# A decoder layer's projection units: even row lengths for the meta operand tiles, another order of the block products, stores by halves

## The chip, the cores and the metric

The kernel runs on one core of a Trainium2 chip. The metric is the device time of one execution in microseconds. The kernel before takes 993.65 us, the median of three runs (993.39 to 994.78).

## What is computed

One layer of a decoder trunk on 1024 tokens and 16 learned meta tokens in front of them, 1024 channels, all in float32:

```
h = rms_norm(h_res, pre_norm_g)
z = h @ w_in                                  # 1024 x 7328
(pv, pg, cq, ckv, kr, mg, cu, cg, sbcx, sg, gl) = split_cols(z)
y_a = (pool_mixer(pv) * silu(pg)) @ w_out_pool
y_b = (mla_attention(cq, ckv, kr) * silu(mg)) @ w_out_mla
y_c = (conformer_conv(cu) * silu(cg)) @ w_out_conf
y_d = (short_conv(sbcx) * silu(sg)) @ w_out_sc
gts = sigmoid(gl + gate_bias)                 # four gates of 1024 channels
m = gts[0]*y_a + gts[1]*y_b + gts[2]*y_c + gts[3]*y_d
h_res = h_res + rms_norm(m @ w_o, post_norm_g)
```

The convolution branch starts with a gated linear unit: `a, gate = split(cu)`, `a * sigmoid(gate)`, then a causal depthwise convolution of width 31, a layer norm and a swish. The meta tokens are dropped at the end.

## The kernel before, in words

The kernel has three stages: the input projection with all that can be made from it beside (about 643 us), attention with three of the output projections, and the last projections with the norm. The change touches the first stage only.

Float32 products are made on TensorE from operands split in two float32r parts, high and low: high·high, high·low and low·high are summed in PSUM, three matmuls for each 128 rows of the contraction. The helper `split` (line 482) makes such a pair: ScalarE copies the high part, POOL subtracts to get the low one.

The projection uses a scheme of seven block products instead of eight (`unit`, line 601). The contraction of 1024 is cut into two halves of 512, 256 output channels into two blocks of 128, and the tokens into two halves. The seven operand tiles of h (B11, T2, T1, T3, B21, T4, B22) are made once, at the start, and stay in SBUF for the whole stage. For every 256 output channels `prep` (line 570) loads the weight columns and makes seven weight blocks (A11, S2, S1, S3, A12, A22, S4) with additions on VectorE and a split of each (`blk`, line 563). One block product is 12 matmuls (`product`, line 586): four steps of the contraction, three matmuls each. The weight block is the stationary operand, the operand tile the moving one.

An operand tile is stored as [128, 2, 4, row]: high and low, four steps, and a row. Three tiles (T1, T3, B22, the list `BARE`) have rows of 512 floats, 2048 bytes. The four others (B11, T2, B21, T4) hold 16 meta columns behind the 512 tokens: rows of `LH` = 528 floats, 2112 bytes. A weight block is stored as [128, 4, row] with the high part in a row's first 128 floats and the low part in the next 128. Blocks that meet a tile with meta columns (`SKEW`: A11, S2, A12, A22) have 16 more floats, rows of 1088 bytes, and a ring of four buffers; the others have rows of 1024 bytes and a ring of three.

A unit sums into four PSUM banks, ps_pa to ps_pd, in this order: A11·B11 in ps_pa; S2·T2 in ps_pb; S1·T1 in ps_pc; S3·T3 on top of ps_pb; A12·B21 on top of ps_pa; A22·T4 in ps_pd; S4·B22 on top of ps_pc. Between them ScalarE copies ps_pa into a buffer `a_`, VectorE forms u2 and u3 from ps_pb and `a_`, and four result blocks leave through the function `out(i, j, ...)`, with i the block of 128 channels and j the half of the tokens: (1,1) from ps_pc and u3 after S3·T3, (0,0) from ps_pa after A12·B21, (1,0) from ps_pd and u3 after A22·T4, and (0,1) from ps_pc and u2 after S4·B22. There are 28 pairs of 128 channels (`pairs`, line 1227). Five need the meta tokens as well and run as two units of 256 and 256 + 16 columns each, and 23 run as one unit of 512 columns. Of those, 16 are merge gates (`out_gate`: one tanh with a bias), five are SiLU paths (`out_silu`: a tanh into a scratch tile and a product on VectorE) and two are plain (`out_tok`). Both halves of a channel block are gathered in a z tile of two buffers and stored to DRAM in one transfer, the merge gates' from ScalarE's queue (the last pair's from POOL's), the others' from SP's queue.

Beside the units run side tasks, four lanes of generators (line 1207) that `pump` moves on after each product, at a pace written beside each lane: the convolution, the attention's keys, values and queries, the short convolution, pooling and norms, and the splits of later weights. `task_conv` loads a and gate from DRAM, makes the gated product (a tanh of 542 columns on ScalarE and a product on VectorE), and then 31 multiply-adds on VectorE.

All instructions are recorded first. `Plan.flush` (line 352) then places them with a list of costs: each engine takes, of the recorded work whose operands, buffers and banks are free by its estimate, the one of the highest priority. So the order on each engine is the planner's, and what the chip does differently from the estimate shows as a wait. Every instruction passes through `issue`, so that its line in the profile is 350 throughout; instructions are told apart by tile names.

## Time and profile before

| | |
|---|---|
| median of three runs | 993.65 us (993.39 to 994.78) |
| profiled execution | 994.93 us |
| its span, first to last instruction | 993.2 us |
| granted TensorE clock, mean | 0.994 |
| TensorE busy | 971.4 us, 98%, 5093 matmuls |
| VectorE, ScalarE, POOL busy | 691.2, 446.4, 693.7 us |
| DMA | 203 MB, 205 GB/s over the span |
| projection stage ends, attention's first matmul | 643 us |

The profile lists busy time by engine, groups of equal instructions, the waits, and a chain: from the last instruction back, at each step, to what released it. A matmul's listed duration (some 390 ns at 512 columns) overlaps the next one's; the distance between starts is read from the chain, where a run of matmuls into one bank stands with its start, its length in time and its count. PE is TensorE, DVE is VectorE, ACT is ScalarE; SPq and ACTq are queues that issue DMAs.

### The profile page before, as it was taken

To read this page: it belongs to the slowest core of one execution; us is meant where nothing else is said; L and a number is where in the kernel's file an instruction comes from. 1 tells how busy PE (TensorE), PEld (TensorE's weight loads), DVE (VectorE), ACT (ScalarE), POOL (GpSimd) and SP (SyncE) were. 2 spreads that over 40 slices of the span, in tenths; PEclk is the share of its full clock that TensorE was granted. 3 is DMA by queue.
4 is the path that set the end of the run, shared out by engine and by line. 5 is a ranking of instruction groups with operands and counts; after the bars stand their busy time and mean duration, and the time that the engine had idled before them with its cause. 6 is when DMAs were issued, how large, how long until landed. Compare 5 with 4: busy or idle time off the path is not lost.

```text
span 993.2 us, 15194 instructions
## 1 busy us (share of the span) xinstructions
PE 971.4 (98%) x5093; PEld 823.4 (83%) x5093; DVE 691.2 (70%) x1105; ACT 446.4 (45%) x894; POOL 693.7 (70%) x638
## 2 busy tenths in 40 slices
PE   9999999999999999999999999979999999999996
PEld 9999898889888888888888888858888878788885
DVE  6944796997899589545565453266777787799547
ACT  7633234453345454545443444215665546224632
POOL 5866978667677767758876685235569886656956
PEclk9999999999999999999999999999999999999998
DMA  7268755678675976755745746795758672673534
GB/s 252 77 205 282 271 164 177 206 224 295 228 252 181 311 233 192 245 180 174 243 141 181 212 159 191 292 255 177 212 150 252 200 221 76 245 251 108 183 116 169
DMA packets 126878, 203.13 MB, mean 205 GB/s; under 512 B 19650, under 2 KB 79161, under 8 KB 126032
## 3 DMA queue, kind: packets, MB, share of 16 engines
q1 hardware_dynamic: 122176, 185.38, 59.2%
q10 hardware_dynamic: 4336, 15.73, 4.2%
q8 instruction: 40, 0.66, 0.3%
q0 software_dynamic: 288, 1.05, 0.3%
q14 instruction: 38, 0.31, 0.1%
HBM read 128.40 MB, written 73.72 MB: 204 GB/s over the span
## 4 chain that ended last, share of the span: by engine, by line
PE 92%; DVE 4%; DMA 2%; issue 1%; POOL 1%; ACT 0%; SPq 0%; DVEq 0%; POOLq 0%; ACTq 0%
PE ps_pa L350 16%; PE ps_pb L350 16%; PE ps_pc L350 15%; PE ps_o L350 10%; PE ps_pd L350 7%; PE ps_s L350 7%; PE ps_y L350 7%; PE ps_u L350 7%; PE ps_x L350 4%; PE ps_w L350 1%; DMA kt<-kr 1%; DVE ps_w L350 1%; DVE op L350 1%; DVE a L350 0%; DVE m L350 0%
## 5 line engine op out<-in xcount | busy, mean ns | idle before, releaser
L350 PE MATMUL ps_pa<-B,A 128*128 128x512 f32 (+2 forms) x792 | 172.8, 361 | 0.0
L350 PE MATMUL ps_pb<-T,S 128*128 128x512 f32 (+2 forms) x792 | 170.9, 359 | 0.0
L350 POOL TENSOR_TENSOR S<-ss,S 128x512 fp32r<-128x512 f32 x84 | 117.5, 1411 | 61.1 <-ACT S L350 60.8
L350 POOL TENSOR_TENSOR A<-raw,A 128x512 fp32r<-128x512 f32 x84 | 118.3, 1415 | 50.2 <-ACT A L350 45.1
L350 PEld LDWEIGHTS ps_pa<-B,A 128*128 128x128 f32 x792 | 133.8, 188 | 23.4 <-issue 1.4
L350 PEld LDWEIGHTS ps_pb<-T,S 128*128 128x128 f32 x792 | 133.7, 188 | 21.9
L350 POOL TENSOR_TENSOR pt<-p,pt 128x512 fp32r<-128x512 f32 (+4 forms) x112 | 104.0, 955 | 50.4 <-PE ps_s L350 39.1
L350 DVE SCALAR_TENSOR_TENSOR ps_w<-conv,par,ps_w 128x512 f32<-128x512 f32 x116 | 87.2, 752 | 2.5
L350 PE MATMUL ps_pd<-T,A 128*128 128x512 f32 (+2 forms) x396 | 85.7, 361 | 0.0
L350 ACT ACTIVATE S<-ss 128x512 fp32r<-128x512 f32 x84 | 52.4, 631 | 72.5 <-PE ps_pc L350 37.0
L350 PE MATMUL ps_pc<-B,S 128*128 128x512 f32 (+1 forms) x396 | 84.3, 359 | 0.0
L350 PE MATMUL ps_pc<-T,S 128*128 128x512 f32 (+1 forms) x396 | 84.2, 359 | 0.0
L350 ACT ACTIVATE p<-ps_s 128x512 f32<-128x512 f32 (+4 forms) x112 | 49.7, 444 | 75.2 <-PE ps_s L350 30.1
L350 PE MATMUL ps_y<-bo,whl 128*128 128x512 f32 x288 | 81.6, 402 | 0.1
L350 PEld LDWEIGHTS ps_pd<-T,A 128*128 128x128 f32 x396 | 67.3, 188 | 11.7
L350 PEld LDWEIGHTS ps_pc<-B,S 128*128 128x128 f32 x396 | 66.9, 188 | 11.7 <-issue 0.5
L350 PEld LDWEIGHTS ps_pc<-T,S 128*128 128x128 f32 x396 | 66.7, 188 | 11.7 <-issue 0.5
L350 PE MATMUL ps_o<-pt,vt 128*128 128x512 f32 (+4 forms) x336 | 73.6, 334 | 2.6 <-ACT ol L350 2.4
L350 ACT ACTIVATE A<-raw 128x512 fp32r<-128x512 f32 x84 | 52.7, 628 | 32.2 <-PE ps_pd L350 21.6
L350 PE MATMUL ps_s<-qt,kt 100*128 100x512 f32 (+4 forms) x336 | 66.1, 325 | 0.7 <-DVE qt L350 0.7
L350 PEld LDWEIGHTS ps_o<-pt,vt 128*128 128x128 f32 (+1 forms) x336 | 52.5, 173 | 15.8 <-ACT ol L350 3.7
L350 PEld LDWEIGHTS ps_s<-qt,kt 100*128 100x128 f32 (+1 forms) x336 | 53.8, 176 | 11.3 <-issue 0.9
(341 smaller groups left out, 1897.3 us busy)
## 6 DMA issues: line engine op xcount, KB each, us to landing
raw<-in_w_in_dram SPq DMA_DIRECT2D x56, 512.0 KB
th<-th SPq DMA_DIRECT2D x32, 512.0 KB
th<-z ACTq DMA_DIRECT2D x30, 512.0 KB
v<-vhl SPq DMA_DIRECT2D x16, 384.0 KB
qt<-q SPq DMA_DIRECT2D x16, 384.0 KB
vt<-v SPq DMA_DIRECT2D x8, 768.0 KB
bo<-bo SPq DMA_DIRECT2D x6, 1024.0 KB
kt<-k SPq DMA_DIRECT2D x8, 520.0 KB
```

Of the source, the lines that this page charges most:

```text
L350: getattr(self.handle[o["eng"]], o["op"])(*map(real, o["args"]), **{k: real(v) for k, v in o["kw"].items()})
```

## The change

Operand tiles with meta columns get rows of `LR` = 576 floats (2304 bytes). All weight blocks get one layout [128, 2, 4, 128], high part and low part apart, in rows of 512 bytes, and share one ring of seven buffers. In `unit` the products A12·B21 and A22·T4 change places (outside the very first pair's units, where A12·B21 runs early as before). The buffer `a_` is dropped: u3 holds the copy of ps_pa, and the scratch of a SiLU's block (1,1) is ps_pb. Result halves are stored on their own for SiLU, plain and gate pairs, with three z buffers instead of two. The two pairs of the gated unit are regrouped so that each holds 128 channels of a and the 128 channels of its gate; `out_glu` makes the gated product as the blocks leave, only that is stored, and the convolution task loads it ready. It runs its 31 steps from the last to the first and ends in place. The pace of the lane with keys, values and queries is 0.9 instead of 0.8.

```diff
-LK = 1088
+LK, LR = 1088, 576
-SKEW = ("A11", "S2", "A12", "A22")
...
-        HB[b] = hpool.tile([P, 2, KH, 512 if b in BARE else LH], F32R, name=name)
+        HB[b] = hpool.tile([P, 2, KH, 512 if b in BARE else LR], F32R, name=name)
...
     def blk(src, name):
-        skew = name in SKEW
-        b = wp.tile([P, KH, 2 * P + 16 * skew], F32R, tag="blks" if skew else "blk", bufs=3 + skew, name=name)
-        hi, lo = b[:, :, :P], b[:, :, P:2 * P]
-        split(hi, lo, src)
-        return hi, lo
+        b = wp.tile([P, 2, KH, P], F32R, tag="blk", bufs=7, name=name)
+        split(b[:, 0], b[:, 1], src)
+        return b
...
-            PE.matmul(ps, w[0][:, k], xh, start=start and k == 0, stop=False, skip_group_check=True)
+            PE.matmul(ps, w[:, 0, k], xh, start=start and k == 0, stop=False, skip_group_check=True)
...
-        a_ = up.tile([P, 512], F32, tag="a", name="a_")[:, :n]
...
             with plan.ahead(EVAC):
-                out(0, 0, pa, None, u3 if early else a_)
+                out(0, 0, pa, None, u3)
...
-            copy(a_, pa)
+            copy(u3, pa)
...
-            add(DVE, u2, pb, a_)
+            add(DVE, u2, pb, u3)
...
-            add(DVE, u3, pb, a_)
-            out(1, 1, pc, u3[:, :nb], a_)
+            add(DVE, u3, pb, u3)
+            out(1, 1, pc, u3[:, :nb], pb)
         pump()
-        if not early:
-            first()
         product(pd, w["A22"], T4, c0, n, True, True)
         with plan.ahead(EVAC):
             out(1, 0, pd, u3, u3)
         pump()
+        if not early:
+            first()
...
+    def out_glu(name, c0, n):
+        z, place = pairs_of(n)
+        k = min(n, 512 - c0)
+        def out(i, j, ps, x, tmp):
+            second = i in z
+            full(place(i, j, ps), x, ps)
+            if second and i:
+                for h in range(2):
+                    g = z[1][:, h, :n if h == 0 else k]
+                    ACT.activation(g, g, AF.Tanh, scale=0.5)
+            elif second:
+                for h in range(2):
+                    g, u = (z[e][:, h, :n if h == 0 else k] for e in (1, 0))
+                    DVE.scalar_tensor_tensor(u, g, 1.0, u, op0=ALU.add, op1=ALU.mult)
+                store_both(name, z[0], c0, n)
+        return out
...
     def out_tok(names):
-        return pairs_of_halves(512, lambda i, to, ps, x, tmp: full(to, x, ps),
-                               lambda i, t: SP.dma_start(z_dram[names[i]], row(t)))
+        return halves_of(512, lambda i, to, ps, x, tmp: full(to, x, ps),
+                         lambda i, j, t: SP.dma_start(half(z_dram[names[i]], j), t))
...
-        return pairs_of_halves(512, each, lambda i, t: (POOL if g == 30 else ACT).dma_start(th_dram[g + i], row(t)))
+        return halves_of(512, each, lambda i, j, t: (POOL if g == 30 else ACT).dma_start(half(th_dram[g + i], j), t))
...
     def wload(i, c, n=2 * P):
         t = raw("raw")
-        SP.dma_start(t[:, :, :n], w_in[:, KH * i:KH * (i + 1), c:c + n])
+        for e, c_ in enumerate(c if isinstance(c, tuple) else (c,)):
+            m = P if isinstance(c, tuple) else n
+            SP.dma_start(t[:, :, P * e:P * e + m], w_in[:, KH * i:KH * (i + 1), c_:c_ + m])
         return t
...
     def task_conv(m, c):
         n = 512 + 30
-        t = tp.tile([P, 2, n], F32, tag="conv", bufs=1, name="conv")
-        g, th, out = t[:, 0], t[:, 1], t[:, 1, :512]
+        g = tp.tile([P, n], F32, tag="conv", bufs=1, name="conv")
...
-        ld(th[:, z0:], z_dram[f"g{m}"][:, n0 + z0:n0 + n])
-        ACT.activation(th[:, z0:], th[:, z0:], AF.Tanh, scale=0.5)
-        yield
-        DVE.scalar_tensor_tensor(g[:, z0:], th[:, z0:], 1.0, g[:, z0:], op0=ALU.add, op1=ALU.mult)
         yield
-        for t in range(31):
+        for t in reversed(range(31)):
...
-             ): 0.8,
+             ): 0.9,
...
-        (C_CU, ("a0", "a1"), MT),
-        (C_CU + 256, ("g0", "g1"), MT),
+        ((C_CU, C_CU + 256), ("a0",), GLU),
+        ((C_CU + P, C_CU + 256 + P), ("a1",), GLU),
```

81 lines of the change are left out of this document (45 added, 36 removed).

## The prediction

> **What bounds the kernel now.** I read the page's busy times first, then the chain of work that ended last, then a table by stage, then the chain again in short windows. The busy times and the chain's shares by engine:
>
> ```profile
> PE 971.4 (98%) x5093; PEld 823.4 (83%) x5093; DVE 691.2 (70%) x1105; ACT 446.4 (45%) x894; POOL 693.7 (70%) x638
> PE 92%; DVE 4%; DMA 2%; issue 1%; POOL 1%; ACT 0%; SPq 0%; DVEq 0%; POOLq 0%; ACTq 0%
> ```
>
> TensorE carries 92% of the chain. The table by stage (columns: length, then PE, PEld, DVE, ACT and POOL busy with counts, granted clock, DMA share, GB/s), for one stretch near the start and one near the end of the projection stage, which is the only stage that the change touches:
>
> ```profile
> 25.00:75.00 50.00, 50.00 (x425) 49.53 (x424) 35.07 (x62) 26.08 (x56) 36.20 (x30) 1.00 0.45 142
> 575.00:625.00 50.00, 50.00 (x219) 40.74 (x218) 22.90 (x30) 22.89 (x38) 37.08 (x28) 1.00 0.61 185
> ```
>
> TensorE has no idle time there and the clock is full, so this stage is as long as its matmuls are apart, and a nanosecond off each of them counts. How far apart they are is seen in the chain, which gives each run of twelve matmuls (one block product) its start, length and count. This is the last unit of 512 columns before attention:
>
> ```profile
> 623.70 2.76 PE ps_pa L350 x12
> 626.45 2.78 PE ps_pb L350 x12
> 629.23 2.74 PE ps_pc L350 x12
> 631.98 2.72 PE ps_pb L350 x12
> 634.70 2.76 PE ps_pa L350 x12
> 637.45 2.78 PE ps_pd L350 x12
> 640.23 2.74 PE ps_pc L350 x12
> 642.98 0.55 PE ps_s L350 x4
> ```
>
> In the old order these are A11·B11, S2·T2, S1·T1, S3·T3, A12·B21, A22·T4, S4·B22. All do the same arithmetic on the same shape, and yet they take 2.72 to 2.78 us. The four at 2.76 and 2.78 are those whose operand tile has rows of 528 floats, 2112 bytes (8 x 256 and 64 over), with a weight block in rows of 1088 bytes (4 x 256 and 64 over). The three at 2.72 and 2.74 have rows of 2048 and 1024 bytes. Of these S3·T3, which follows another even product, has 2.72; the two in ps_pc, which both follow a shifted one (T2, T4), have 2.74. The last stage works on even rows only, 96 matmuls at a time:
>
> ```profile
> 907.35 21.76 PE ps_o L350 x96
> ```
>
> That is 2.72 us for twelve: the pace where nothing is shifted.
>
> **The change, part by part.** *Rows of 2304 bytes (9 x 256), weight halves in rows of 512.* Now every operand and every weight block of the units starts its rows on the same step. How many units there are comes from the groups by shape, 24 matmuls a unit in ps_pa:
>
> ```profile
> L350 PE MATMUL ps_pa<-B,A 128*128 128x512 f32 x552 | 139.6, 395 | 0.0
> L350 PE MATMUL ps_pa<-B,A 128*128 128x272 f32 x120 | 17.0, 288 | 0.0
> L350 PE MATMUL ps_pa<-B,A 128*128 128x256 f32 x120 | 16.1, 280 | 0.0
> ```
>
> So 23 units of 512 columns, five of 256 and five of 272. A unit of 512 lasts 642.98 - 623.70 = 19.28 us. With all seven products at 2.72 it is 19.04: 0.24 less, and 23 x 0.24 = 5.5 us less on the path. If the ps_pc products stayed at 2.74 it would be 0.20 and 4.6 us. I take 5.5, because S3·T3 is of the same form as the two in ps_pc and differs from them by what ran just before it.
>
> The small units go the other way. One of 256 columns, from the same view:
>
> ```profile
> 114.01 1.41 PE ps_pa L350 x12
> 115.42 1.39 PE ps_pb L350 x12
> 116.81 1.42 PE ps_pc L350 x12
> 118.23 1.44 PE ps_pb L350 x12
> 119.67 1.41 PE ps_pa L350 x12
> 121.08 1.39 PE ps_pd L350 x12
> 122.47 1.42 PE ps_pc L350 x12
> 123.90 0.50 PE ps_pb L350 x4
> 85.50 1.50 PE ps_pa L350 x12
> 91.74 1.53 PE ps_pd L350 x12
> ```
>
> Here the even S3·T3 is the slowest, 1.44, and the shifted ones have 1.39 to 1.41. Seven at 1.44 are 10.08 against 123.90 - 114.01 = 9.89: 0.19 more, five times, +1.0 us. For 272 columns (the last two rows are of such units) no even product exists. From 1.44 at 256 and 2.72 at 512 I estimate 1.44 + 16/256 x 1.28 = 1.52. The unit is then 4 x 1.52 + 3 x 1.44 = 10.40, against about 10.33 (four at 1.50 to 1.53 and three at 1.42 to 1.44): five times +0.07, +0.3 us; bounds 0 and +1.0, what the units of 256 lose. Rows in all: -5.5 + 1.0 + 0.3 = -4.2 us, between -2.6 (-4.6 + 1.0 + 1.0) and -4.5.
>
> *A22·T4 ahead of A12·B21.* The number of matmuls stays. The wait that becomes tighter is that for ps_pa: A12·B21 ends in it, and the next unit's A11·B11 begins in it. Two products lay between them, now only S4·B22, which is 2.72 us (1.44 in small units). Whoever empties ps_pa later than that stops TensorE with all that is queued on it. The evictions, with the products that they follow or that run meanwhile:
>
> ```profile
> 637.49 0.69 ACT L350 ACTIVATE z<-ps_pa,par 128x512 f32<-128x512 f32 x1 [0.58 <-PE ps_pa L350]
> 256.98 2.78 PE ps_pd L350 x12
> 259.23 0.68 DVE L350 SCALAR_TENSOR_TENSOR z<-a__3131,ps_pa 128x512 f32<-128x512 f32 x1
> 66.55 1.51 PE ps_pa L350 x12
> 70.63 0.38 ACT L350 ACTIVATE z<-ps_pa 128x272 f32<-128x272 f32 x1
> 56.56 1.39 PE ps_pa L350 x12
> 58.04 0.39 ACT L350 ACTIVATE z<-ps_pa 128x256 f32<-128x256 f32 x1 [2.04 <-PE ps_pa L350]
> ```
>
> A merge gate's is done at 638.18, 0.7 us after A12·B21 gave way at 637.45: 2 us to spare in 16 units. A SiLU unit empties ps_pa in two steps, and VectorE ends the second at 259.91, 2.9 us after 256.98: 0.2 us too late, in five units. There the tanh of ps_pa also goes into u3, which the block before it must have read: that chain is an add (0.69), a tanh (0.64) and a product (0.68) after A22·T4, inside A12·B21's 2.72 but with little over. Small units: one eviction ended at 58.43, some 0.5 us after its product, and one at 71.01, 2.95 us after 68.06, because ScalarE had other work or the z buffer was not free. Bounds for all of this are 0 and, with 1.5 us in each of the ten small units and 0.5 in the five SiLU units, 17 us. The order of the changed program puts S2·T2 of the next unit, or matmuls of the side tasks, between A12·B21 and the next A11·B11 behind all five SiLU units and behind two of the small ones, and there are now three z buffers instead of two, so I take a value near the lower end: +0.4 for small units, +0.2 for SiLU units.
>
> *Blocks stored by halves.* ScalarE issues 60 stores instead of 30, POOL four instead of two, SP eight DMAs more in all (halves of SiLU and token stores and two loads for each gated pair, less the gate's round trip through DRAM).
>
> ```profile
> L350 ACTq DMA_DIRECT2D th<-z x30: 326/326/379, 321.7 to 625.2; - x30
> DMA to landing us min/median/max: 3.1/3.8/4.6
> ```
>
> 30 x 0.33 = 10 us more on ScalarE's queue, spread over 300 us in which it is under half busy: nothing. Four halves a unit share three buffers. The first is ready 2.2 us after S3·T3 ends (two adds of 0.69 and a gate tanh of 0.73), its store lands by +0.3 and at most 4.6 (landings of the same tensor's loads and stores), 7.1 us after S3·T3. The fourth half is wanted 3 x 2.72 = 8.2 us after it. If that cover is gone, VectorE stands, and with it the next u2; TensorE notices after a further 5 us (S1·T1 waits for ps_pc). Cost taken: 0.
>
> *The gated unit.* Eight tanh and eight products of 256 to 272 columns in the first two pairs replace four and four of 542 columns in the convolution task. They lie in the stretch 25:75 and the one behind it, where VectorE has 15 us of 50 free; without that cover they would cost 8 x 0.8 = 6 us. The removed loads and stores of g relieve a DMA system that bounds nothing here. In SiLU units ps_pb is the scratch of a tanh after S3·T3: its next writer, S2·T2, comes three or four products (8 to 11 us) later. One ring of seven weight buffers instead of rings of four and three holds the same seven blocks: nothing. The side lane's pace of 0.9 instead of 0.8 moves its matmuls earlier, not their number: nothing.
>
> *Behind the stage.* Attention and the output stage keep their order on TensorE, so what is won is kept if the first loads of attention move with it.
>
> ```profile
> 669.67 0.78 PE L350 MATMUL ps_s<-kt,qt 96*128 96x144 f32 x2 [5.50 <-DMA kt<-kr]
> ```
>
> This wait of 5.5 us is for a load that is issued behind TensorE's and VectorE's own progress, so I let it move along.
>
> **The sum.** -5.5 + 1.0 + 0.3 + 0.4 + 0.2 = -3.6 us. The profiled execution took 994.93 us (span 993.2), which makes 991.3; it stands 1.3 above the median of the three runs, 993.65, and against that the forecast is 990.0 us.
>
> **Rivals.** *Rows do not matter* (same). The 0.04 to 0.06 us could belong to the PSUM banks or to the place in the unit instead of the rows: pd and the first use of pb are the slow ones, in every unit. For it: the banks are confounded with the operands. Against it: pb has both 2.78 (T2) and 2.72 (T3). Then only the hand-off is left, 993.65 + 0.6 = 994.3. [...]
>
> *Won and waited away* (same): the load of kt lands when it landed before, and TensorE waits 5.5 + 3.6 us for it: 993.7. For it: the wait exists. Against: its issue is behind the stage.
>
> *ps_pa stops TensorE* (slower): the hand-off above, at the start of A11·B11. It decides once its sum over all units passes 4.2 + 2.0 us, that is 0.2 us in each of 33 units, or 0.6 in each of the ten small ones. For it: of the quoted evictions the one at 71.01 and the SiLU one would be late. With 0.4 us a unit it is 33 x 0.4 = 13.2: 993.65 - 4.2 + 13.2 = 1002.7 us.
>
> **How the numbers follow.** 0.2%, 2 us, is about what a measurement of this kernel can tell from no change. The forecast has 0.68, and its own range is 989.2 (rows at their best, no stall) to 991.6; rows without effect 0.11; waited away 0.05; ps_pa 0.16, of which a mild form ends within 0.2%, say 0.02. So faster 0.68, same 0.18, slower 0.14. The range reaches over the cases without change (994.3) into the slower one and leaves out half of that; below, 2 us are left for the spread of the runs (993.39 to 994.78) and for a row count that falls under 2.72: 987.2 to 996.0.
>
> **What would show it.** In the changed kernel's chain, each product of 512 columns at 2.72 and a unit at 19.04; products of 256 at 1.44; the start of attention some 3.6 us earlier than 642.98; ps_pa never as a wait before A11·B11 in gate units. Wrong would be: 2.76 or 2.78 still there, gaps before ps_pa ended by ACT or DVE, idle time of VectorE ended by a z store, or a longer wait for kt.

## The result, and the profile after

The changed kernel takes 1000.11 us, the median of six runs (996.97 to 1001.63), against 994.13 us (993.02 to 994.91, six runs) for the kernel before in the same comparison: a ratio of 1.0054 with a 95% interval of 1.0035 to 1.0073. The forecast was 990.0 us, with a range up to 996.0. The profiled execution took 1000.41 us, its span is 998.7 us, 5.5 us more than before. One of all the runs below, r_act's at 1067.59 us with a mean granted clock of 0.848, was in a slower state and is left out of its ratio.

Busy times and the chain's shares by engine, from the page of the changed kernel:

```profile
PE 972.7 (97%) x5093; PEld 826.4 (83%) x5093; DVE 691.4 (69%) x1109; ACT 444.5 (45%) x898; POOL 690.7 (69%) x640
PE 86%; POOL 4%; DVE 4%; issue 3%; DMA 2%; ACT 1%; SPq 0%; ACTq 0%; DVEq 0%; POOLq 0%
```

The work is the same, but TensorE's share of the chain fell from 92% to 86%: other engines now end waits, and the chain then runs along their work ahead of the wait, so that the six points are more than the waits themselves. The chain of the last unit before attention, and some products of 256 and 272 columns (start, length, engine, tile, count):

```profile
113.11 1.43 PE ps_pa L349 x12
...
123.27 1.50 PE ps_pa L349 x12
...
624.76 2.72 PE ps_pa L349 x12
627.48 2.72 PE ps_pb L349 x12
630.20 2.72 PE ps_pc L349 x12
632.92 2.72 PE ps_pb L349 x12
635.64 2.72 PE ps_pd L349 x12
638.36 2.72 PE ps_pa L349 x12
641.08 2.72 PE ps_pc L349 x12
643.80 0.55 PE ps_s L349 x4
```

Every product of this unit is at 2.72, the unit at 643.80 - 624.76 = 19.04 us, as the forecast had it; a unit of 256 columns takes 123.27 - 113.11 = 10.16 us, where it had 10.08. Yet attention begins at 643.80 instead of 642.98. Added up from start to start over the whole stage in the two profiled executions (idle time of more than 0.06 us counted as a wait), the products of 512 columns took 447.1 us before and 443.8 after, those of 256 columns 71.1 and 72.1, those of 272 columns 30.3 and 30.4, all other matmuls 92.3 and 91.7, and the waits 0.5 and 4.2: -3.3 + 1.0 + 0.0 - 0.6 + 3.7 = +0.8 us. The 512-column term is smaller than the unit above suggests, because it is an undisturbed one. Of the 161 products of 512 columns 111 run without another matmul in between (108 before), and their mean fell from 2.756 to 2.725 us; the others have matmuls of the side tasks in them and took 2.82 us before and 2.83 after.

Which waits these are is in the summary of TensorE's waits from 75 to 643 us (total in us, times, longest). Before:

```profile
PE ps_x L350 <- DVE rs L350: 0.4, 1, 0.4
```

After:

```profile
PE ps_x L349 <- POOL rs L349: 2.6, 2, 2.0
PE ps_x L349 <- DVE rs L349: 1.0, 2, 0.7
PE ps_y L349 <- POOL rs L349: 0.4, 1, 0.4
```

That is 4.0 us of waits instead of 0.4 (the sum above also counts those too short for this list). None is for ps_pa or a z buffer. All are for the row sums `rs` of the side lanes: VectorE scales them, POOL raises them to the power -1/2, TensorE transposes them. The two at POOL, as TensorE's timeline has them, in the changed kernel:

```profile
160.62 0.95 PE L349 MATMUL ps_x<-ones,sqk 128*128 128x1 f32 x8
...
165.74 0.65 PE L349 MATMUL ps_x<-ident,rs 128*128 128x128 f32 x4 [1.97 <-POOL rs L349]
...
170.21 0.65 PE L349 MATMUL ps_x<-ident,rs 128*128 128x128 f32 x4 [0.63 <-POOL rs L349]
```

And what VectorE did between the sums (done at 161.6) and their scaling at 164.43:

```profile
154.33 2.73 DVE L349 TENSOR_TENSOR ss<-raw,ss 128x512 f32<-128x512 f32 x1
156.99 4.70 DVE L349 SCALAR_TENSOR_TENSOR ps_w<-conv,par,ps_w 128x512 f32<-128x512 f32 x6
161.60 0.68 DVE L349 TENSOR_TENSOR u<-ps_pb,u 128x512 f32<-128x512 f32 x1
162.20 2.33 DVE L349 SCALAR_TENSOR_TENSOR ps_w<-conv,par,ps_w 128x512 f32<-128x512 f32 x3
164.43 0.15 DVE L349 TENSOR_SCALAR rs<-ps_x 128x4 f32<-128x4 f32 x1
```

VectorE works without a pause, on the convolution's multiply-adds and on one weight addition that took 2.73 us. The convolution finds its gated product ready, so its first multiply-add starts at 97.6 us instead of 118.1. In the table by stage VectorE's busy time from 75 to 125 us rises from the first row (before) to the second (after):

```profile
75.00:125.00 50.00, 50.00 (x342) 46.47 (x341) 31.29 (x45) 14.19 (x29) 39.78 (x30) 1.00 0.83 274
```

```profile
75.00:125.00 50.00, 50.00 (x340) 46.63 (x340) 44.32 (x68) 14.68 (x32) 33.85 (x27) 1.00 0.73 248
125.00:175.00 50.00, 47.40 (x332) 43.81 (x331) 41.49 (x60) 16.39 (x33) 38.92 (x29) 1.00 0.55 176
```

The second loss is behind the stage. From attention's first matmul to the end it takes 998.7 - 643.8 = 354.9 us, where it took 993.2 - 643.0 = 350.2, although TensorE's order there is the same. Laid one over the other, matmul by matmul, the two executions part at three places. The wait for kt is shorter, 3.22 us instead of 5.50, but after it the clock stays low longer. Then a new wait stands at 816.45, and a low clock behind it. The rows of the changed kernel, from TensorE's timeline:

```profile
668.14 0.78 PE L349 MATMUL ps_s<-kt,qt 96*128 96x144 f32 x2 [3.22 <-DMA kt<-kr]
816.45 0.27 PE L349 MATMUL ps_s<-ident,mr 128*4 128x128 f32 x1 [2.84 <-DVE mr L349]
```

Its table by stretch (the column behind the five engines is the granted clock):

```profile
667.50:677.50 10.00, 9.36 (x30) 7.94 (x31) 5.06 (x13) 1.70 (x3) 0.00 (x0) 0.50 0.34 101
677.70:680.00 2.30, 2.30 (x11) 1.88 (x10) 0.00 (x0) 2.24 (x5) 2.25 (x2) 1.00 0.53 205
817.60:820.90 3.30, 3.30 (x9) 2.56 (x8) 3.23 (x8) 0.10 (x1) 0.00 (x0) 0.50 0.62 236
```

And of the kernel before:

```profile
666.40:673.00 6.60, 3.33 (x13) 3.15 (x13) 0.81 (x3) 0.00 (x0) 0.00 (x0) 0.50 0.59 158
673.20:676.00 2.80, 2.80 (x16) 2.38 (x16) 2.09 (x5) 0.70 (x2) 0.00 (x0) 1.00 0.00 0
```

After the wait for kt the changed kernel works 677.6 - 668.1 = 9.5 us at half clock, the kernel before 673.1 - 669.7 = 3.4: 6 us more at half speed cost about 3. The wait at 816.45 is 2.6 us longer than the 0.24 that stood there before, and some 3.4 us of half clock behind it cost 1.7. So -2.3 + 3 + 2.6 + 1.7 = 5, which is the 4.7 within the coarseness of these rows. Read from the starts of the single matmuls, the four steps are -2.35, +2.67, +2.49 and +1.41 us, and 0.44 us comes in small steps.

What ended the wait at 816.45 is an addition on VectorE of two operands in SBUF, beside six POOL instructions without a gap. VectorE and POOL in the changed kernel:

```profile
810.02 5.42 DVE L349 TENSOR_TENSOR m<-m,th 128x512 f32<-128x512 f32 x1
...
810.03 2.41 POOL L349 TENSOR_TENSOR pt<-p,pt 128x400 fp32r<-128x400 f32 x4
812.40 2.48 POOL L349 TENSOR_TENSOR m<-m,th 128x512 f32<-128x512 f32 x2
```

The same instructions before:

```profile
808.97 2.82 DVE L350 TENSOR_TENSOR m<-m,th 128x512 f32<-128x512 f32 x1
...
809.01 2.86 POOL L350 TENSOR_TENSOR pt<-p,pt 128x400 fp32r<-128x400 f32 x4
811.84 2.49 POOL L350 TENSOR_TENSOR m<-m,th 128x512 f32<-128x512 f32 x2
```

The usual length of this addition is 0.80 us (the median of 32). Before, it ended together with POOL's first four, one of which took 0.45 us longer: VectorE got in between. After, it stood until all six were done, 0.6 us past 814.88.

### The profile page after: what moved, and what is told of

Same layout as the page of the kernel before. It is cut to its first block, busy times and chain, and to the rows that moved or that the text cites. A ratio compares the mean times of both kernels' runs of the same rounds, so it can differ in the third digit from the quotient of the medians.

```text
span 998.7 us, 15346 instructions
## 1 busy us (share of the span) xinstructions
PE 972.7 (97%) x5093; PEld 826.4 (83%) x5093; DVE 691.4 (69%) x1109; ACT 444.5 (45%) x898; POOL 690.7 (69%) x640
## 4 chain that ended last, share of the span: by engine, by line
PE 86%; POOL 4%; DVE 4%; issue 3%; DMA 2%; ACT 1%; SPq 0%; ACTq 0%; DVEq 0%; POOLq 0%
PE ps_pa L349 15%; PE ps_pb L349 14%; PE ps_pc L349 13%; PE ps_o L349 10%; PE ps_s L349 7%; PE ps_pd L349 7%; PE ps_y L349 7%; PE ps_u L349 7%; PE ps_x L349 4%; POOL S L349 1%; PE ps_w L349 1%; POOL A L349 1%; DMA kt<-kr 1%; DVE m L349 1%; POOL rs L349 1%
## 5 line engine op out<-in xcount | busy, mean ns | idle before, releaser
L349 PE MATMUL ps_pa<-B,A 128*128 128x512 f32 (+2 forms) x792 | 170.0, 359 | 0.0
L349 POOL TENSOR_TENSOR S<-ss,S 128x512 fp32r<-128x512 f32 x84 | 113.7, 1366 | 59.8 <-ACT S L349 57.1
L349 POOL TENSOR_TENSOR A<-raw,A 128x512 fp32r<-128x512 f32 x84 | 112.6, 1350 | 38.9 <-ACT A L349 36.9
L349 DVE TENSOR_TENSOR u<-ps_pb,u 128x512 f32<-128x512 f32 (+2 forms) x66 | 40.3, 610 | 80.4 <-PE ps_pb L349 77.7
L349 ACT ACTIVATE S<-ss 128x512 fp32r<-128x512 f32 x84 | 50.3, 627 | 66.3 <-DVE ss L349 46.1
```

What stands on the lines that cost most here:

```text
L349: getattr(self.handle[o["eng"]], o["op"])(*map(real, o["args"]), **{k: real(v) for k, v in o["kw"].items()})
```

## The experiments

The theory at the start: the rows give what was forecast, and VectorE's queue gives it back in waits, because the convolution now starts earlier; the rest is the two events in attention. Rivals: rows do not matter; the lane's pace; the hand-off of ps_pa; waits that only change place. The table has every kernel that was run, in the order of the runs: median, ratio to the kernel before with its interval, start of attention's first matmul in the profiled execution, and from there to the end of its span.

| run | edit, on which kernel | us | ratio | attention at | rest |
|---|---|---|---|---|---|
| before | | 993.5 to 994.1 | | 642.8 | 350.4 |
| after | | 1000.11 | 1.0054 (1.0035 to 1.0073) | 643.6 | 355.1 |
| r_rows | after, old rows | 1001.34 | 1.0075 (1.0059 to 1.0091) | 644.3 | 354.8 |
| r_pace | after, lane at 0.8 | 1016.09 | 1.0224 (1.0209 to 1.0240) | 645.5 | 369.7 |
| r_late | after, convolution recorded later | 996.49 | 1.0032 (1.0019 to 1.0045) | 641.0 | 351.7 |
| r_order2 | after, old order of products | 1002.03 | 1.0087 (1.0068 to 1.0105) | 644.4 | 354.2 |
| r_noglu | after, old gated pairs | 1028.81 | 1.0359 (1.0337 to 1.0382) | 669.9 | 359.1 |
| r_bpace | before, lane at 0.9 | 993.25 | 1.0002 (0.9988 to 1.0016) | 642.0 | 350.4 |
| r_addpool | after, additions on POOL | 999.10 | 1.0055 (1.0033 to 1.0076) | 646.6 | 351.8 |
| r_brows | rows without the rest | 998.47 | 1.0040 (1.0025 to 1.0055) | 642.2 | 356.2 |
| r_rsahead | after, rs at higher priority | 1012.88 | 1.0192 (1.0172 to 1.0211) | 643.1 | 367.0 |
| r_lateadd | r_late and r_addpool | 992.85 | 0.9994 (0.9981 to 1.0007) | 640.9 | 349.1 |
| r_badd | before, additions on POOL | 995.69 | 1.0018 (1.0006 to 1.0030) | 641.3 | 350.8 |
| r_ss | r_lateadd, one subtraction on POOL | 993.30 | 0.9989 (0.9974 to 1.0003) | 640.9 | 351.7 |
| r_na | after, 29 of 31 multiply-adds left out | 994.09 | 1.0006 (0.9992 to 1.0021) | 640.5 | 351.5 |
| r_nr | r_na with old rows | 998.51 | 1.0044 (1.0031 to 1.0057) | 643.1 | 354.7 |
| r_nb | before, the same left out | 1003.89 | 1.0106 (1.0089 to 1.0122) | 644.1 | 353.0 |
| r_conv8 | r_lateadd, convolution at 0.8 | 1003.17 | 1.0085 (1.0069 to 1.0100) | 641.2 | 359.3 |
| r_act | r_addpool, rs on ScalarE | 996.77 | 1.0029 (1.0015 to 1.0044) | 644.1 | 350.9 |
| r_best | r_ss, rs on ScalarE | 992.19 | 0.9989 (0.9976 to 1.0001) | 639.7 | 350.9 |

The last two columns are one execution each, from the first matmul's own start, which the group rows give 0.2 us ahead of the chain's piece. r_badd has the projection stage of the kernel before, and r_addpool that of the changed kernel: 641.3 beside 642.8, and 646.6 beside 643.6. A difference under 1.5 us in these columns says nothing by itself, and I go by the rows of the waits where I can.

**Old rows in the changed kernel (r_rows).**

```diff
-LK, LR = 1088, 576
+LK, LR = 1088, 528
+        skew = name in SKEW
+        b = wp.tile([P, KH, 2 * P + 16 * skew], F32R, tag="blks" if skew else "blk", bufs=3 + skew, name=name)
```

> Everything of the change stays, only the rows go back: operand tiles in rows of 2112 bytes, the four weight blocks that meet them in rows of 1088. My theory is that the rows give what was forecast, 0.04 to 0.06 us for each product of 512 columns, and that something else of the change takes it away again. Then the products of 512 columns are at 2.76 and 2.78 again, the projection stage ends 4.2 us (bounds 2.6 to 4.5) later than the changed kernel's 643.80, at about 648, and the kernel takes some 1004 us. The rival, that rows do not matter or that TensorE waits for something else at the same pace, expects 643.8 and 1000 us.

Its chain has the old paces back at once, in the same places, for the same tiles:

```profile
625.17 2.76 PE ps_pa L350 x12
627.92 2.78 PE ps_pb L350 x12
...
636.17 2.76 PE ps_pd L350 x12
638.92 2.78 PE ps_pa L350 x12
```

The order of the products is that of the changed kernel, in whose unit above every one took 2.72 us, so it is the rows, not the place or the bank. (ps_pd and ps_pa have changed places since the kernel before and their 2.78 and 2.76 with them; that finer difference goes with the place.) But the stage is only 0.7 us longer, not 4.2, and 644.3 and 1001.34 us are nearer to the rival's 643.8 and 1000 than to the theory's 648 and 1004: TensorE's waits in it fell to 1.7 us. So the rows have their price, and in the changed kernel most of what they give is waited away.

**The lane's pace alone (r_pace).**

```diff
-             ): 0.9,
+             ): 0.8,
```

> One number of the change goes back: the pace of the lane with keys, values and queries is 0.8 again. If that pace is what set the lane's row sums among the convolution's steps on VectorE (theory pace), the waits of TensorE for POOL's rs at 165.74 and 170.21 (2.1 and 0.8 us) and the later ones of the same form (some 2 us) go, and attention begins near 640. If it is the convolution that starts a pair earlier (theory convolution), the lane meets it at 0.8 as well: waits of 1 to 3 us of that form stay, at other places, and attention begins between 642.5 and 645.

The wait at 166 stays (2.08 us), so the pace did not make it. Attention begins 0.5 us behind the bounds of theory convolution. What nobody expected is that the rest takes 14.6 us longer, at the start of attention. TensorE's timeline has a wait of 2.44 us for a z, and then:

```profile
657.74 2.47 PE L349 MATMUL ps_y<-bo,whl 128*128 128x512 f32 x5 [8.42 <-DMA whl<-w_out_pool]
```

The last of the query stores is issued at 630.8 here, at 607.5 in the changed kernel and at 597.0 before. Attention's loads come behind it: in the chain the transfer qt<-q stands for 9.85 us from 631.53, and right behind it whl<-w_out_pool for 16.21 us from 641.39. In this order the pace of 0.9 keeps the lane's end ahead of attention.

**The convolution recorded a pair later (r_late; in the expectations: the late convolution).**

```diff
-        lane(*[((f"a{m}",), task_conv, m, c) for c in range(2) for m in range(2)]): 0.9,
+        lane(*[(("a0", "a1"), task_conv, m, c) for c in range(2) for m in range(2)]): 0.9,
```

> The convolution waits for both channel pairs (a0 and a1) as it did before, so that it starts after the second pair and not after the first; all else of the change stays. Theory convolution: the waits for rs at 165.74 and 170.21 go, attention begins 2.9 us earlier than 643.80, near 641 (bounds 640 to 642). Theory pace: they stay, 643 to 645. For attention and the last stage (354.9 us in the changed kernel, 350.2 before) neither says anything; if the wait at 816 and the two long drops of the clock are a matter of the exact moments, they may go with this edit, which would give 350 to 352 and a time of 992 to 996.

The waits for rs are gone and attention begins 2.6 us earlier, as theory convolution had it; the 996.49 us lie just over the 996 that were named. But the convolution does not start later on the chip. The edit has its tasks recorded a pair later, so that they rank lower in the planner's list; their data are there as early, and the first multiply-add starts at 98.1 us. The multiply-adds (after the colon: shortest, median and longest in ns, first and last start in us) and the scaling of the keys' row sums, in the changed kernel:

```profile
L349 DVE SCALAR_TENSOR_TENSOR ps_w<-conv,par,ps_w x116: 735/756/757, 97.6 to 326.9; 128x512 f32<-128x512 f32 x116
L349 DVE TENSOR_SCALAR rs<-ps_x x3: 139/155/155, 164.4 to 175.1; 128x4 f32<-128x4 f32 x2, 16x1 f32<-16x1 f32 x1
```

In r_late, with its row of the table by stage:

```profile
L349 DVE SCALAR_TENSOR_TENSOR ps_w<-conv,par,ps_w x116: 732/756/757, 98.1 to 343.9; 128x512 f32<-128x512 f32 x116
L349 DVE TENSOR_SCALAR rs<-ps_x x3: 138/161/162, 145.3 to 153.0; 128x4 f32<-128x4 f32 x2, 16x1 f32<-16x1 f32 x1
75.00:125.00 50.00, 50.00 (x340) 46.66 (x340) 43.84 (x67) 15.14 (x32) 39.25 (x31) 1.00 0.80 265
```

VectorE is as busy from 75 to 125 us as in the changed kernel (43.84 us beside 44.32). What moved is the order: the row sums are scaled at 145.3 to 153.0, ahead of the convolution's second task, and no longer at 164.4 to 175.1, in the midst of it. So the order on VectorE makes these waits; the early start and the fuller stretch alone do not. A new wait stands in their place:

```profile
139.83 0.50 PE L349 MATMUL ps_pb<-T,S 128*128 128x256 f32 x2 [1.55 <-DVE u L349]
```

VectorE came late with `u` because it stood 3.87 us (from 135.57) in the subtraction ss<-raw,ss beside POOL. The long addition in attention is there as well, 5.44 us, with a wait of 2.86 behind it.

**The old order of products (r_order2).**

```diff
+        if not early:
+            first()
         product(pd, w["A22"], T4, c0, n, True, True)
...
-        if not early:
-            first()
```

> A12·B21 stands ahead of A22·T4 again, the scratch of a SiLU's block (0,0) is the result tile itself; all else of the change stays. The rival of the prediction, that the tighter hand-off of ps_pa stops TensorE, expects attention to begin 4 us or more earlier than 643.80. My theory is that the hand-off costs no more than the 0.6 us that I gave it: 642.5 to 644.5, with the waits for rs still there.

Attention at 644.4, a wait of 2.53 us for rs at 166.75 with 3.4 us of half clock behind it, and one of 1.51 for `u` at 595. The hand-off of ps_pa is not the cause; that rival falls.

**The gated pairs as before (r_noglu).**

```diff
-        ((C_CU, C_CU + 256), ("a0",), GLU),
-        ((C_CU + P, C_CU + 256 + P), ("a1",), GLU),
+        (C_CU, ("a0", "a1"), MT),
+        (C_CU + 256, ("g0", "g1"), MT),
...
+        th = t2([P, n], name="th")
```

> The two pairs of the gated unit are as before (a0, a1 and then g0, g1, stored raw), and the convolution task loads both, makes the gated product itself and so starts after the second pair; all else of the change stays. If the gated product in the output of the first units costs nothing, as predicted, attention begins where it did with the late convolution alone, at 641.2 (bounds 640.5 to 642). If it is this work on VectorE that stops TensorE around 140 (1.7 us at 139.83 in the run with the late convolution), attention begins near 639.5 (bounds 638.8 to 640.2), which is all that the rows were to give.

Inconclusive for its question, since the gate's tile was put into a ring that the other lane shares, and the last norm then ended behind the stage; kt is waited for 23.07 us. One thing it does tell: waits for `u` on VectorE sum to 2.9 us here without the gated product, so that product is not what made them.

**The pace in the kernel before (r_bpace).**

```diff
-             ): 0.8,
+             ): 0.9,
```

> The kernel before with one number of the change: the lane with keys, values and queries at a pace of 0.9 instead of 0.8. Theory convolution: the convolution still starts late here, so no wait for rs of over 1 us appears near 165 to 190, attention begins at 643 (bounds 642 to 644), and the last store of the queries comes earlier than 597.0. Theory pace: waits of 1 to 3 us of that form appear, and attention begins at 644 to 646.

Only one wait for rs, 0.5 us; 993.25 us, no change. Theory pace falls, and the last query store is issued at 570.7: in the old order the pace only shifts work.

**Attention's additions on POOL (r_addpool).**

```diff
-                        add(POOL if bi == 1 else DVE, m_[c][d], m_[c][d], t)
+                        add(POOL, m_[c][d], m_[c][d], t)
```

> The changed kernel with the additions m<-m,th of the third output projection on POOL instead of VectorE; the projection stage is untouched. If the wait of 2.8 us at 816.45 comes from VectorE's addition standing 5.42 us beside POOL's (port), then without it that wait and the 3.41 us of half clock behind it go, and from the start of attention to the end it takes 354.9 - 2.8 - 1.5 = 350.6 us (bounds 349.5 to 352), the kernel some 996 us. If the wait only moves, to another wait for VectorE or POOL, 354 to 356 and 1000 us.

"Port", here and in later expectations, is a name for my guess that VectorE's instruction stands because POOL works beside it; no run shows what the two share. The rest took 351.8 us, inside the bounds, and the wait at 816 is gone. But another has come, for `th` on VectorE, with 3.4 us of half clock behind it (867.1 to 870.5). VectorE stands 3.48 us in two products of SBUF operands, which took 1.27 us in the kernel before (at 815.51), beside six of the additions that POOL now does; `th` is behind them in its queue. VectorE, POOL and TensorE:

```profile
861.63 3.48 DVE L349 TENSOR_TENSOR op<-ol,rb 64x512 f32<-64x512 f32 x2
...
856.48 7.48 POOL L349 TENSOR_TENSOR m<-m,th 128x512 f32<-128x512 f32 x6
...
865.86 0.43 PE L349 MATMUL ps_y<-ident,ol 64*128 64x64 f32 x4 [2.13 <-DVE th L349]
```

The planner's order in attention is another one too: 1489 of TensorE's 1644 matmuls behind the stage keep their place. Counted from attention's first matmul, this execution is 5.6 us ahead of the changed kernel at 818 us, 6.2 at 849, 2.6 at 871 and 3.3 at the end. So VectorE's standing beside POOL was moved and not removed; the new wait and its half clock take back 3.6 us, and that the rest met a forecast without them is in part luck. The same wait (2.13 to 2.17 us) stands in r_lateadd, r_badd, r_ss, r_act and r_best, and one of 2.40 us for `th` in r_conv8. The total moved by 1 us only, since in this execution the unchanged wait near 166 was followed by some 6.8 us of half clock (table by stretch):

```profile
167.50:174.10 6.60, 6.60 (x21) 5.18 (x22) 6.24 (x11) 0.00 (x0) 3.57 (x4) 0.50 0.18 60
```

In the changed kernel's own profile the same wait (1.97 us at 165.74) left the clock at 1.00 (from 165.7 to 175.0). So one wait can cost its 2 us, or 2 and 3 more. That runs of one kernel lie up to 5 us apart fits this, but only the profiled ones show their clock by stretch.

**The rows without the rest (r_brows).**

```diff
+LK, LR = 1088, 576
+        b = wp.tile([P, 2, KH, P], F32R, tag="blk", bufs=7, name=name)
...
-        a_ = up.tile([P, 512], F32, tag="a", name="a_")[:, :n]
```

> The rows without the rest: operand tiles in rows of 2304 bytes, weight blocks in rows of 512 in one ring of seven, and what makes room for them (u3 instead of a_, three z buffers and stores by halves). The order of the products, the two pairs of the gated unit, the convolution task with its tanh and product (its gate held in a z buffer) and the pace of 0.8 are those of before. Theory: the rows are worth 4.2 us (2.6 to 4.5) wherever VectorE answers as it did before; attention begins at 638.8 (638.5 to 640.5), and the kernel takes 989 to 992 us. The rival, that TensorE gains on VectorE and waits for it whatever the rest is, expects waits of 2 us and more in the stage and attention at 641 to 643.5, with 993 to 996 us.

Attention at 642.2: the rival's number, not the theory's. Waits of 3.6 us stand in the stage, the largest 1.64 at 133.78, behind this pair on VectorE and POOL:

```profile
128.72 4.20 DVE L349 TENSOR_TENSOR raw<-raw 128x512 f32<-128x512 f32 x1
...
128.21 2.91 POOL L349 TENSOR_TENSOR krl<-kr,krh 32x1040 fp32r<-32x1040 f32 x1
131.09 2.96 POOL L349 TENSOR_TENSOR S<-ss,S 128x512 fp32r<-128x512 f32 x2
```

Here the convolution starts about as late as before (116.5). So such waits need no early convolution: with other buffers the planner writes another order, and in it VectorE's additions meet POOL's work without a gap. In the kernel before, the longest of the four weight additions' 112 took 1.80 us. The planner counts 142 + 1.07 x 512 = 690 ns for one and something for POOL's turn (`cost`, `turns`), not 4.2 us.

**Row sums at a higher priority (r_rsahead).**

```diff
-        DVE.tensor_scalar(rs, pc, 1.0 / of, EPS, op0=ALU.mult, op1=ALU.add)
+        with plan.ahead(4000):
+            DVE.tensor_scalar(rs, pc, 1.0 / of, EPS, op0=ALU.mult, op1=ALU.add)
```

> The changed kernel, with the row sums' instructions (rs on VectorE and POOL) placed with a priority of 4000 more, so that the planner puts them ahead of the convolution's multiply-adds; all else stays. If the queue on VectorE is what TensorE waited for at 165.74 (2.1 us) and 170.21 (0.8), these waits fall under 0.5 us each and attention begins 2 to 3 us earlier than 643.80, at 641 to 642. If it is POOL's pow or the transfer of ckv before it, the waits stay: 643 to 645.

A miss: VectorE's order around 164 came out the same, and the wait too. Elsewhere it changed, the last query store slid to 625.9, and attention waited 7.59 us for whl, as in r_pace.

**Both that helped (r_lateadd).** Its edit is that of r_late and that of r_addpool.

> The late convolution and the third projection's additions on POOL together, all else of the change as it is. By the sum of what both did alone: attention at 641.2 as with the late convolution; from there to the end 350.6 (349.5 to 352) without VectorE's wait of 2.5 to 2.8 us beside POOL and the half clock behind it. The kernel then takes 991.8 + 1.3 = 993 us (991.5 to 995), level with the kernel before. If the wait only moves, 996 as with the late convolution alone.

992.85 us, as summed: 7.3 us less than the changed kernel, by two edits neither of which touches the rows. The rest took 349.1 us, 0.4 less than the bounds, although the wait for `th` stands in it (2.16 us at 857.50, with 3.4 us of half clock), which the sum did not have.

**The control for it (r_badd).** The edit of r_addpool in the kernel before.

> The kernel before with the third output projection's additions on POOL and nothing else: the control for the two kernels that moved them. The profiled execution of the kernel before had VectorE's addition at that place at 2.82 us and no wait of TensorE behind it, so by the port theory there is nothing to win: 993.9 us, within 1.5. If the move is a gain by itself, whatever happens at that wait, it shows here as well: 990 to 991.

995.69 us, 0.3 outside the bound, and 1.8 us slower by the ratio, whose interval leaves out 1. The wait for `th` (2.13 us at 859.69, with 3.4 us of half clock) stands here too, and did not before. So the move of the additions has a price of its own, and is a gain where it takes away the long addition's wait. The group of these additions in the kernel before (shortest, median and longest in ns; first and last start):

```profile
L350 DVE TENSOR_TENSOR m<-m,th x32: 689/804/2824, 803.9 to 908.6; 128x512 f32<-128x512 f32 x32
```

In r_late the longest is 5.44 us. In r_lateadd sixteen are left on VectorE, those from 863.9 us on, and the longest of them takes 1.41 us.

Of the executions with before's order in attention and the additions on VectorE, the two with before's first stage have 2.8 us and the seven with a changed one (after, r_rows, r_late, r_order2, r_brows, r_na, r_nr) 5.42 to 5.52. The instructions and their order are the same, and VectorE and POOL start within 0.1 us of each other in all nine. Their places in SBUF are not the same: in the two, this addition's `th` and the last of the four `pt` lie in other buffers of their rings than in any of the seven. No run tells whether that or the moment decides; why VectorE gets in between in the one and not in the other stays open.

**One subtraction moved to POOL (r_ss).**

```diff
-        sub(DVE, s2, a12, s2)
+        preps[0] += 1
+        sub(POOL if preps[0] == 5 else DVE, s2, a12, s2)
```

> Late convolution, third projection's additions on POOL, and one instruction more moved: the subtraction ss<-raw,ss of the fifth set of weight blocks, which stood 3.87 us on VectorE beside POOL's four splits and held back the add into u that TensorE waited for at 139.7, is done on POOL. Port theory: the wait of 1.7 us at 139.7 goes, attention begins at 639.5 (639 to 640.5) and the kernel takes some 991 us (989.5 to 993). If VectorE is simply short of time there, TensorE waits for it a little later: 641 to 642 and 993 us.

The wait at 139.7 is gone; attention begins at 640.9 all the same, with a wait of 0.8 us for `vhl` on VectorE at 327 and others below. The second outcome: it moved on, as far as attention's start tells; the 993.30 us fit it too.

**Less convolution: the changed kernel, with old rows, and the kernel before (r_na, r_nr, r_nb).**

```diff
-            else:
+            elif t == 0:
                 DVE.scalar_tensor_tensor(acc if t else g[:, :512], g[:, t:t + 512], w, acc, op0=ALU.mult, op1=ALU.add)
```

> The changed kernel with 29 of the 31 multiply-adds of the convolution left out (its first and last step stay, and the pauses between steps too), so that VectorE has some 90 us less to do in the projection stage. Theory VectorE: the rows' gain is there, and was waited away only because VectorE could not keep up; then no wait of over 1 us stands between 75 and 640, and attention begins 4 to 5 us earlier than 643.80, at 638.8 to 640. The rival, that TensorE waits for something else (POOL, transfers, banks), keeps 642 to 644.

> The same, and the rows of before (2112 and 1088 bytes) in the kernel that is otherwise the changed one: beside the run without the multiply-adds it differs by the rows alone. Theory VectorE: the stage is longer by the whole price of the rows, 4.2 us (2.6 to 4.5): attention at 643 to 644.5. The rival, that the gain is waited away whatever VectorE has to do, gives less than 1.5 us between the two.

> The kernel before with the same 29 multiply-adds left out. It had only some 2 us of waits for VectorE there, so it has little to win: attention at 641.5 to 643. Beside the changed kernel without them the whole change should then show what was forecast for it in this stage, 3 to 4 us less; the rival gives less than 1.5 us.

These three leave out most of the convolution, so they do not compute the layer; only their times are of use. In r_na no wait of over 0.5 us is left in the summary from 75 to 640 us, and attention begins at 640.5 (the bounds ended at 640), in r_nr at 643.1, in r_nb at 644.1. With 1.5 and 1.4 us of waits in the first two, they differ by the rows alone: 2.6 us, the lower bound of the forecast, and 4.4 in the medians, where the stretches of half clock in attention differ as well. The whole change gives 3.6 us in the stage against r_nb (each start is good to 1.5 us). So with VectorE relieved the stage gets about what was forecast for it. r_nb's own start was expected at 641.5 to 643 and came later; its total is spoilt by a late last store of a side lane (630.3) and waits for whl of 1.08 and 2.79 us.

**A thinner convolution in the whole kernel (r_conv8).**

```diff
-    ... for c in range(2) for m in range(2)]): 0.9,
+    ... for c in range(2) for m in range(2)]): 0.8,
```

> A whole kernel again: late convolution, third projection's additions on POOL, and the convolution's lane at a pace of 0.8 instead of 0.9, so that its multiply-adds lie less dense where the keys' and queries' lane and the weight blocks want VectorE. Theory VectorE: the wait of 1.7 us at 139.7 shrinks and attention begins at 639 to 640.5; 990 to 992 us in all, unless the last tasks of the lane now end too late and hold back attention's first loads, which would show as a longer wait for kt or bo and 993 to 1000 us.

The wait at 139.8 did not shrink (1.6 us), and the lane ended too late: waits of 2.54 us for a z and 3.44 for whl at the start of attention, 1003.17 us. A miss, with the mishap that had been named.

**The scaling on ScalarE (r_act).**

```diff
-        DVE.tensor_scalar(rs, pc, 1.0 / of, EPS, op0=ALU.mult, op1=ALU.add)
+        ACT.activation(rs, pc, AF.Identity, scale=1.0 / of, bias=epsc[:p])
```

> The changed kernel with the third projection's additions on POOL, and one step more: the row sums' scaling (rs<-ps_x, the instruction of VectorE that POOL's power waits for) is done on ScalarE, which is under half busy there. Theory VectorE's queue: the waits of TensorE for rs near 166 and 170 (1.9 us and more) go, with the half clock behind them, and attention begins at 640.5 to 642; with 350.6 from there the kernel takes 992.5 us (991 to 995). If POOL or the transfer before it was late, the waits stay and it takes 997 to 1000 us.

The waits for rs near 166 are gone, and others stand in their place, 3.5 us from 169 to 192, the longest of them (TensorE's timeline):

```profile
169.22 0.62 PE L349 MATMUL ps_x<-ident,rs 128*128 128x128 f32 x4 [1.12 <-DVE ckv L349]
```

Attention begins at 644.1 and not at 640.5 to 642, and 996.77 us is 1.8 over the bounds. So it was VectorE's queue, and taking one instruction off it hands the wait to the next one; three of the four waits are for VectorE, one of 0.9 us is for ScalarE.

**All that helped (r_best).** The edits of r_ss and r_act.

> All that helped, together: late convolution, third projection's additions on POOL, the one subtraction of the fifth weight set on POOL, and the row sums' scaling on ScalarE. Theory VectorE's queue: the remaining waits for VectorE (0.8 and 0.4 us) shrink, attention begins at 639 to 640.5 and the kernel takes 990 to 992 us, ahead of the kernel before. If VectorE's shortage only moves on, 641 and 993 us as before.

Attention at 639.7 and 992.19 us (990.74 to 994.77): the first whole kernel whose stage is shorter than before's by more than the rows gave (3.1 us). Its waits in the stage are 0.8 us. Its interval still touches 1: it can't be told from the kernel before. Of the 3.1 us won up to attention 2.6 are left in the span, and 1.6 in the medians.

## Why the prediction was wrong, point by point

*Rows.* The paces were right, to the hundredth: 2.72, 19.04 for an undisturbed unit, and 1.44 for small products; 272 columns took 1.50 where 1.52 was estimated, so the +0.3 was 0.0. The term "23 x 0.24 = 5.5 us" was too large: it takes every product of 512 columns for undisturbed, and the third of them that has side matmuls in it gained nothing (2.82 us before, 2.83 after). These products gave 3.3 us, and the rows in all -3.3 + 1.0 + 0.0 = -2.3 us instead of -4.2; the 2.6 us between r_na and r_nr agree. That the rows and not the banks or the place make the difference is shown by r_rows (2.76 and 2.78 us there, 2.72 in the changed kernel). No run shows how the rows come to cost this.

*Small units, hand-off, stores by halves.* No wait for ps_pa or for a z buffer in the changed kernel's summary: the 0.6 us taken were not spent. The rival "ps_pa stops TensorE" named the right sign and nearly the right total (1002.7) by the wrong mechanism, which is luck; r_order2 rules it out.

*The gated unit: "they lie in the stretch 25:75 and the one behind it, where VectorE has 15 us of 50 free".* This step failed. It weighed the moved tanh and products against VectorE's free time and put what follows from them at nothing. What follows is that the convolution's multiply-adds start 20 us earlier and that, in the planner's order, those of its second task stand on VectorE before the lane's row sums, for which TensorE waits. Free time in a stretch was not the measure either: VectorE's 31.29 us of 50 from 75 to 125 became 44.32, but in r_late and r_best, at 43.84 and 43.82, there are no such waits at 166. The more general fault is earlier in the argument: that the stage is "as long as its matmuls are apart". That held in the order of before, with 0.5 us of waits; the forecast carried it over to another order on VectorE and POOL, and r_brows has 3.6 us of waits without the new gated unit. The missing term is +3.7 us. Against the -3.6 us that were forecast, the stage's +0.8 is then: -2.3 for the rows instead of -4.2, +3.7 for the waits instead of nothing, 0 for the hand-off instead of +0.6, and -0.6 for the other matmuls, which the sum left out. That is so in these two executions; r_addpool shows that the same stage can take 3 us more in another.

*The pace: "moves its matmuls earlier, not their number: nothing".* In the old order this holds (r_bpace: 993.25 us). In the changed one the pace is worth 16 us: without it the lane's end is late and the kernel takes 1016.09 us.

*Behind the stage: "what is won is kept", the wait for kt "moves along".* This step failed too, by 4.7 us. The wait for kt became 2.3 us shorter, so it does not move along; but the time at half clock behind it and the wait at 816.45 with its own half clock took more. r_lateadd gets 3.6 us back from r_late by moving sixteen additions, the long one among them, from VectorE to POOL, where r_badd gains nothing. What is shown is that VectorE stands beside POOL's instructions (5.42 us), that TensorE waits behind it (2.84 us), and that the clock falls (to 0.50 for 3.4 us); r_addpool shows that it then stands at another place. That this change would set it off could not be read from the trace before, beyond the one addition of 2.82 us among 32 of 0.80, which was a warning that I didn't read.

Open: why VectorE gets in between POOL's instructions in the one family of kernels and not in the other, and whether the places of `th` and `pt` have to do with it.

## What to carry to other kernels

A schedule written by a planner is tuned as a whole: when TensorE gets faster by 1%, or a task may start a stage earlier, look at the engine that answers it, its busy share by stage and the longest instance of each of its groups, and not only at TensorE's pace. A group whose longest instance is far above its median (here 2.82 us against 0.80) can mark the place where the next change will wait; here one did. The pace of a side lane is a deadline: ask how long before its reader's start its last store is issued (36 to 46 us were enough here, 15 to 17 us were not).

## What the runs showed of the hardware

*VectorE beside POOL.* An addition of two SBUF operands on VectorE, 0.69 us at its shortest, stood 5.42 us, until the last of six POOL instructions without a gap was done (at 814.88), though it had started 0.01 us ahead of the first of them, which may be too little to tell. So VectorE stood and POOL ran on: its six took 2.41 and 2.48 us. In the kernel before, where the addition took 2.82 us, it ended at 811.79, within 0.1 us of the fourth of the six (811.87). With the additions on POOL, two products of VectorE stood in the same way (3.48 us instead of 1.27 in r_addpool).

*Half clock after short waits.* The clock fell to 0.50 for 3.4 us (changed kernel, behind the wait of 2.84 us at 816.45), for 6.8 us (before, from within the wait of 5.50 us for kt; r_addpool, behind the wait of 1.94 us at 166.49) and for 10.2 us (changed kernel, from within the wait of 3.22 us for kt). Behind the wait for rs at 166 it fell in r_addpool and in r_order2 (2.53 us), and not in the changed kernel (1.97), r_pace (2.08) and r_rsahead (1.95). The longer stretches are two and three times the shortest. No run tells what sets that step, or why the same wait has it in one execution and not in another; a wait of 1.94 us, with matmuls on both sides of it, was enough in r_addpool.
